# Where SBUF buffers begin: all activation and weight buffers of a one-core decoder block at 32 mod 64 bytes

## The chip, the cores and the metric

The program runs on 1 core of one Trainium2 chip. The metric is device time in microseconds (us) for one execution of the whole block, lower is better. Engines are named as in the profile: PE (matrix multiply), PEld (its weight load), DVE (vector), ACT (scalar), POOL (GpSimd), SP (the queue that issues the DMAs).

## The reference

One decoder block in float32, on 512 tokens of width 1024:

```python
mod = silu(c) @ w_ada + b_ada                 # six vectors of 1024: shift, scale, gate, twice
h = rmsnorm(x, norm_mix_w) * (1 + scale_m) + shift_m
z, xbc, dt, u_pool, gates = split(h @ w_in)   # 2048, 3072, 32, 1024, 2048 columns
y_ssd = rmsnorm_by_group(ssd_scan(silu(conv(xbc)), dt) * silu(z)) @ w_branch_ssd
y_pool = causal_multiscale_pool(u_pool) @ w_branch_pool
x = x + gate_m * ((sigmoid(g1) * y_ssd + sigmoid(g2) * y_pool) @ w_out)
h2 = rmsnorm(x, norm_mlp_w) * (1 + scale_f) + shift_f
x = x + gate_f * (square(relu(h2 @ w_up)) @ w_down)   # hidden width 4096
return rmsnorm(x, norm_final_w)
```

## The kernel before, in words

Activations stand channels on partitions, tokens along the row: a tile is 128 partitions by 512 float32, 2,048 bytes in each partition. Every product of float32 operands is made of three products in float32r: each operand is split in a high and a low part (`split`, L107, for activations; `load_unit`, L120, for weights), and `mm3` (L138) adds `whi·xhi`, `whi·xlo` and `wlo·xhi` (L140, L141, L142) into one PSUM bank. A **unit** (L144) is one column block of 128 of a weight with eight chunks of rows: 24 such matmuls, each with 128x128 weights and 512 columns of a moving tile. The moving tile is always an activation part; the weights are always a slice of an `hl` buffer, except in three blocks of the output projection (L689), whose parts stand in `s` buffers.

The stages follow one another: first norm and first units (L198 to L295), the scan in four groups with other units between its steps (L399 to L600), the gates (L606), the last group's branch projection and pooling mix (L618), the pooling branch's projection (L623), the second gates (L630), the output projection (L681 by whole rows of 512 tokens, L691 by halves of 256), and the MLP (L734 on; the last three blocks by halves, L747).

Buffers come from rings (`Slots`, L40): `s0` to `s49` of 2,048 bytes, `raw0` to `raw3` and `hl0` to `hl7` of 4,096, `xs0`, `xs1`, `sz0`, `sz1` of 8,192, `mt0` to `mt2` of 4,096, and `sm0` to `sm3` of 16 bytes. A ring hands its buffers out in the order in which they came back, so which buffer a tile gets is fixed when the program is built. SBUF addresses are given in the order in which the buffers are first made, each rounded up to 32 bytes. The fixed tiles of L85 to L103 come first; the rings follow when each buffer is first asked for. In the program before, `sm0` (16 bytes, rounded up to 32) is first asked for in the first norm, when `s0` to `s15` have an address and `s16` to `s49` have none. So two families stand in the program:

| buffers | address mod 64 bytes, before | after |
|---|---|---|
| `xs`, `sz`, `raw0`, `s0` to `s15` | 0 | 32 |
| `raw1` to `raw3`, all `hl`, `s16` to `s49`, `mt` | 32 | 32 |
| `cbc`, `ident`, `ones` | 0 | 32 |
| `mod`, `tri` | 32 | 0 |
| `ea`, `dtk`, `ncs`, `cd`, `dec` | 0 | 32 |
| `par_t` | 0 | 0 |

The second row's buffers begin at 288 mod 512 before and at 416 mod 512 after: all of them move by the same 128 bytes. The first row's move by 160 bytes. `s0` to `s15` are called the low buffers below. Of the 24 moving tiles of a unit, the low ones number:

| stage | time in the profile before, us | matmuls of 512 columns | low moving tiles in a unit of 24 |
|---|---|---|---|
| three groups' branch projection, in the scan | 164 to 377 | 24 blocks of 12 | 3 in a block of 12 |
| last group's branch projection | 461 to 479 | 8 blocks of 12 | 6 in a block of 12 |
| pooling branch projection | 505 to 550 | 8 units | 9 |
| second gates | 550 to 593 | 8 units | 0 |
| output projection, first five blocks | 593 to 621 | 5 units | 8 |
| MLP, whole rows | 658 to 979 | 58 units | 7, 9 or 11 |

All other units have none: their moving tiles are `h`, in `s17` to `s39`.

Of the kernel before, what the change touches and what calls it, by code (L numbers as in the profile page):

```python
# [7 lines left out]
F32 = mybir.dt.float32  # L8
# [4 lines left out]
P = 128  # L13
# [7 lines left out]
EPS = 1e-5  # L21
WINS = (2, 4, 8, 16)

# Columns of the packed per-channel parameters.
COLS = {}
_n = 0
for _name, _w in (
# [5 lines left out]
NPAR = _n  # L33
# [4 lines left out]


class Slots:  # L40
    """Buffers of one size, handed out in the order in which they were given back."""

    def __init__(self, make, n):
        self.make = make
# [14 lines left out]
def block_kernel(tc, xT, crow, arow, par, adaT, wstart, wz, wx, wpool_in, wgate, wpw, wbs, wbp, wout, wup, wdn, out):  # L59
# [3 lines left out]
    with (  # L63
# [15 lines left out]
        RAW = slots("raw", NRAW, (P, 1024))  # L79
        HL = slots("hl", NHL, (P, 1024))  # L80
        SM = slots("sm", 4, (P, NC))
        PU, PS = slots("ps", 8, (P, T), psp), slots("ps", 8, (P, T), psp)
        PU.free, PS.free = PU.free[:NPU], PS.free[NPU:]

        par_t = sb.tile([P, NPAR], F32, name="par_t")  # L85

        def col(name, j=0, n=1, rows=P):
            a = COLS[name] + j
# [16 lines left out]
        ecs_d = dr.tile([NH, T], F32, name="ecs_d")  # L105

        def split(src):  # L107
            """A tile of float32 in two parts that float32r holds exactly."""
            hi, lo = S.get(F32R), S.get(F32R)
            act.copy(hi, src)  # L110
            dve.tensor_tensor(lo, src, hi.bitcast(F32), ALU.subtract)  # L111
            return hi, lo
# [5 lines left out]
        urgent = [False]  # L118

        def load_unit(src, n=1024, low=None, at=None, cols=1024):  # L120
            """Blocks of 128 columns of a weight, each in two parts; the buffers are free after their next use."""
            at = at or HL
            with tc.high_priority() if urgent[0] else nullcontext():
                r = RAW.get()
                sp.dma_start(r[:, :n], src)
                blocks, kept = [], []
                for a in range(0, n, cols):
                    w = min(cols, n - a)
                    hi, lo = at.get(F32R), at.get(F32R)
                    act.copy(hi[:, :w], r[:, a:a + w])  # L130
                    (low or dve).tensor_tensor(lo[:, :w], r[:, a:a + w], hi[:, :w].bitcast(F32), ALU.subtract)  # L131
                    blocks += [(hi[:, o:o + P], lo[:, o:o + P]) for o in range(0, w, P)]
                    kept += [hi, lo]
            RAW.put(r)
            at.put(*kept)
            return blocks
# [5 lines left out]
            pe.matmul(ps, wlo, xhi[:, t0:t1], start=False, stop=stop)  # L142

        def unit(src, xs):  # L144
            """One column block of 128 with eight chunks of rows; its bank is the caller's to free."""
            w = load_unit(src)
            ps = PU.get()
            for k in range(8):
                mm3(ps, w[k], xs[k], k == 0, k == 7)
            return ps  # L150

        def ada(j, at=RAW):
            """Modulation of 128 channels: silu(c) . w_ada + b_ada."""
            r = at.get()
            sp.dma_start(r, adaT[j])
            dve.tensor_tensor_reduce(r, r, cbc, 1.0, col("b_ada", j), ALU.mult, ALU.add, mod[:, j:j + 1])  # L156
            at.put(r)

        def column_sums(ps, sqs, c0, c1, opened=False):
            """Sums over the partitions of the tiles' chunks of tokens, tokens on partitions."""  # L160
            if len(sqs) == 1 and not opened:
                for c in range(c0, c1):
                    pe.matmul(ps[:, c:c + 1], sqs[0][:, c * P:(c + 1) * P], ones[:, :1], start=True, stop=True)
                return
            if not opened:
                pe.matmul(ps[:, c0:c1], ones, zeros[:, c0:c1], start=True, stop=False)
            for i, sq in enumerate(sqs):
                for c in range(c0, c1):
                    pe.matmul(ps[:, c:c + 1], sq[:, c * P:(c + 1) * P], ones[:, :1], start=False,
                              stop=i == len(sqs) - 1 and c == c1 - 1)  # L170

        def rstd(sums, n, c0, c1, at):
            """1/sqrt(mean + eps) of those sums, on every partition; the bank is the caller's to free."""
            r, d = SM.get(), at.get()
            act.activation(r[:, c0:c1], sums[:, c0:c1], AF.Sqrt, bias=eps_t, scale=1.0 / n)
            dve.reciprocal(r[:, c0:c1], r[:, c0:c1])
            for c in range(c0, c1):
                dc, rc = d[:, c * P:(c + 1) * P], r[:, c:c + 1]
                if c % 2:
                    act.activation(dc, ident, AF.Copy, scale=rc)  # L180
                else:
                    dve.tensor_scalar(dc, ident, rc, None, ALU.mult)
            bc = PU.get()
            pe.matmul(bc[:, c0 * P:c1 * P], ones, d[:, c0 * P:c1 * P], start=True, stop=True)
            SM.put(r)
            at.put(d)
            return bc

        def modulate(x, R, scale, shift, hi, lo, t0=0, t1=T):
            """x * R * scale + shift, in two parts."""  # L190
            t = S.get()
            dve.scalar_tensor_tensor(t[:, t0:t1], x[:, t0:t1], scale, R[:, t0:t1], ALU.mult, ALU.mult)
            act.activation(hi[:, t0:t1], t[:, t0:t1], AF.Identity, bias=shift)
            dve.scalar_tensor_tensor(
                lo[:, t0:t1], t[:, t0:t1], shift, hi[:, t0:t1].bitcast(F32), ALU.add, ALU.subtract)
            S.put(t)

# [1 line left out]
        dve.memset(ones, 1.0)  # L199
        dve.memset(zeros, 0.0)  # L200
        dve.memset(eps_t, EPS)
# [2 lines left out]
            tri, ones, pattern=[[1, P]], compare_op=ALU.is_ge, fill=0.0, base=0, channel_multiplier=-1)  # L204

        def warm(n):
            """Products of no use that keep the array's clock up."""
            ps = PU.get()
            for _ in range(n):
                pe.matmul(ps[:, :P], ones, ones, start=True, stop=True)  # L210
            PU.put(ps)
# [3 lines left out]
        with tc.manual_schedule():  # L215
# [3 lines left out]
            xs0 = [S.get() for _ in range(8)]  # L219
            for k in range(8):  # L220
                sp.dma_start(xs0[k], xT[k])
            sp.dma_start(par_t, par)
            warm(6)
            act.activation(crow_t, crow_t, AF.Silu)
            cps = [PU.get(), PU.get()]
# [27 lines left out]
            R = rstd(ps, DM, 0, NC, S)  # L253
# [40 lines left out]
        PU.put(*first[8 - NPU:])  # L294
        PS.put(*first[1:8 - NPU])  # L295

# [1 line left out]
        r_ = slice(0, NH)  # L298
        w_ = NC * NH
        v, cs_t, ecs_t = S.get(), S.get(), S.get()  # L300
# [35 lines left out]
        PU.put(tk)  # L336
        S.put(v, cs_t, ecs_t, *tmp)

# [1 line left out]
        def conv(ps, j, o=None):  # L340
            t = S.get()
            w = lambda k: col("conv_w", 4 * j + k)
# [38 lines left out]
        acc = [None] * 8  # L381

        def bs(g, jp):
            """Two column blocks of the SSD branch's projection, the rows of one group."""
            def f():
                w = load_unit(wbs[4 * g + jp])
                for jj in range(2):
                    j = 2 * jp + jj
                    ps = PU.get()
                    for k in range(4):  # L390
                        mm3(ps, w[4 * jj + k], G[g]["y"][k], k == 0, k == 3)
                    if g == 0:
                        acc[j] = S.get()
                        act.copy(acc[j], ps)
                    else:
                        dve.tensor_tensor(acc[j], acc[j], ps, ALU.add)
                    PU.put(ps)
                if jp == 3:
                    free(G[g]["y"])  # L399
            return f  # L400
# [113 lines left out]
            SZ.put(sz)  # L514
            S.put(rg)

# [1 line left out]
        pout = []  # L518
        held = {}

# [50 lines left out]
            u_z(0, i)()  # L571

        def run(g, fillers):
            """One group's scan with other units between its steps."""
            steps = ssd_group(g)
            n = 10
            done = 0
            for k in range(n + 1):
                if k == 9 and g == 3:
                    break  # L580
                alive = next(steps, "end")
                upto = len(fillers) * (k + 1) // (n + 1)
                for f in fillers[done:upto]:
                    f()
                done = upto
                if alive == "end":
                    break
            for f in fillers[done:]:
                f()
            return steps  # L590
# [10 lines left out]
        later = [p_.get() for p_ in (XS, SZ, XS)]  # L601
        F = Slots(lambda i, dt: later[i // 4][:, i % 4, :], 12)

# [1 line left out]
        merged = []  # L605
        for j in range(8):  # L606
            gp = F.get()
# [39 lines left out]
        later = [SZ.get(), SZ.get()]  # L647
        F = Slots(lambda i, dt: later[i // 4][:, i % 4, :], 8)

# [1 line left out]
        x1 = []  # L651
        for j in range(8):
            x = xbig[j // 4][:, j % 4, :]
# [3 lines left out]
        HALVES = ((0, H), (H, T))  # L657

        def residual(ps, j, gate, t0=0, t1=T, sums=True, apart=None):
            """Adds a gated product to x and its squares to the sums."""  # L660
            x = x1[j][:, t0:t1]
            dve.scalar_tensor_tensor(x, ps[:, t0:t1], mod[:, gate + j:gate + j + 1], x, ALU.mult, ALU.add)  # L662
            if not sums:
# [39 lines left out]
        for j in range(45, 48):  # L703
            ada(j)

# [1 line left out]
        def squared(u):  # L707
            dve.tensor_tensor(u, u, u, ALU.mult)  # L708
            p = split(u)
# [8 lines left out]
            return squared(u)  # L718

        def up_first():  # L720
            """The first three units, by halves of the tokens and with the rows' chunks outermost."""
            w = [load_unit(wup[i]) for i in range(3)]
            u = [F.get() for _ in range(3)]
            for t0, t1 in HALVES:
# [107 lines left out]
```

## Time and profile before

| | us |
|---|---|
| median of 3 runs | 1006.45 |
| the runs | 1007.35, 1005.21, 1006.45 |
| span of the profiled execution | 1007.3 |
| the run nearest to that span, taken as the profiled execution's own time | 1007.35 |
| PE busy in the span | 985.8 (98%) |
| DVE busy | 623.2 (62%) |
| ACT busy | 482.6 (48%) |

A busy PE means only that some matmul is in flight: a matmul of 512 columns is shown with some 390 ns, while the next one starts some 230 ns after it. The pace is therefore read from start to start, or from the time that a known number of matmuls takes. In the timeline the first column is the start of an instruction; in a table of stretches the count behind an engine's busy time takes in the one or two instructions that hang over the edges.

### The profile page before, as it was taken

Reading aid. Unit: us, or ns where it says so; the run is one execution under the profiler, and the core shown is the slowest. Engines: PE = TensorE matmul, PEld = TensorE weight load, DVE = VectorE, ACT = ScalarE, POOL = GpSimd, SP = SyncE. Lnnn points to the kernel's source line nnn. Section 1 sums busy time; section 2 is a strip of 40 time slices with the busy share of each in tenths; the row PEclk is TensorE's granted clock in tenths of the full one; section 3 lists DMA queues with packets and bytes.
Section 4 is the critical chain, followed back from the end, with each engine's and each line's share of the span. In section 5 each row is a group of like instructions: output and inputs, shape, how many; then the busy total and the mean of one; then the engine's idle time right before and its main releaser. Section 6 shows DMA issues by size and latency. Waiting matters only on the chain.

```text
span 1007.3 us, 12196 instructions
## 1 busy us (share of the span) xinstructions
PE 985.8 (98%) x4732; PEld 804.1 (80%) x4732; DVE 623.2 (62%) x887; ACT 482.6 (48%) x718; POOL 85.7 (9%) x79
## 2 busy tenths in 40 slices
PE   9799999999999999999999999999999999999997
PEld 7577777878778878788888888988888888888886
DVE  5978777586777776978765655654344334434444
ACT  5277899579648933453422433442133123213342
POOL 3510310211012012210000000000000000000000
PEclk9999999999999999999999999999999999999998
DMA  9725542452344232437886444032323222232302
GB/s 357 273 89 169 145 126 91 123 130 91 94 129 123 89 111 94 133 102 230 266 266 196 154 161 144 2 126 83 105 86 103 97 92 94 94 105 84 105 1 84
DMA packets 58620, 129.55 MB, mean 129 GB/s; under 512 B 4609, under 2 KB 29313, under 8 KB 58562
## 3 DMA queue, kind: packets, MB, share of 16 engines
q1 hardware_dynamic: 58562, 128.77, 40.0%
q8 instruction: 37, 0.61, 0.2%
q14 instruction: 21, 0.17, 0.1%
HBM read 126.53 MB, written 2.23 MB: 128 GB/s over the span
## 4 chain that ended last, share of the span: by engine, by line
PE 76%; ACT 8%; DVE 7%; DMA 4%; issue 2%; POOL 1%; SPq 1%; DVEq 0%; POOLq 0%; ACTq 0%
PE ps L140 24%; PE ps L141 24%; PE ps L142 24%; DMA mt<-cs_d 3%; ACT hl L130 2%; DVE sz L156 1%; DVE xs L156 1%; ACT L432 1%; PE ps L469 1%; ACT L349 1%; PE ps L453 1%; PE ps L280 1%; DVE hl L131 1%; ACT mt L432 1%; PE ps L446 1%
## 5 line engine op out<-in xcount | busy, mean ns | idle before, releaser
L140 PE MATMUL ps<-s,hl 128*128 128x512 f32 (+1 forms) x1272 | 493.4, 388 | 1.3 <-ACT pad L528 1.2
L141 PE MATMUL ps<-s,hl 128*128 128x512 f32 (+1 forms) x1272 | 488.4, 384 | 0.0
L142 PE MATMUL ps<-s,hl 128*128 128x512 f32 (+1 forms) x1272 | 488.2, 384 | 0.0
L130 ACT CAST hl<-raw 128x1024 fp32r<-128x1024 f32 (+1 forms) x161 | 167.2, 1041 | 285.3 <-PE ps L141 282.6
L140 PEld LDWEIGHTS ps<-s,hl 128*128 128x128 f32 x1272 | 238.9, 188 | 53.3 <-issue 3.5
L142 PEld LDWEIGHTS ps<-s,hl 128*128 128x128 f32 x1272 | 239.0, 188 | 50.2 <-issue 1.0
L141 PEld LDWEIGHTS ps<-s,hl 128*128 128x128 f32 x1272 | 239.1, 188 | 49.4 <-issue 1.4
L131 DVE TENSOR_TENSOR hl<-raw,hl 128x1024 fp32r<-128x1024 f32 x153 | 189.1, 1238 | 130.3 <-ACT hl L130 126.0
L662 DVE SCALAR_TENSOR_TENSOR xs<-ps,mod,xs 128x512 f32<-128x512 f32 (+1 forms) x46 | 31.3, 681 | 110.6 <-PE ps L142 110.5
L110 ACT CAST s<-sz 128x512 fp32r<-128x512 f32 x52 | 31.5, 620 | 52.8 <-DVE sz L708 42.1
L156 DVE CUSTOM_DVE_ANT_0 raw<-raw,cbc,par_t 128x1024 f32<-128x1024 f32 x32 | 40.9, 1279 | 21.2 <-DMA raw<-adaT 21.2
L111 DVE TENSOR_TENSOR s<-sz,s 128x512 fp32r<-128x512 f32 x52 | 35.0, 690 | 22.9 <-ACT s L110 22.9
L432 ACT ACTIVATE mt<-mt,ncs 128x128 f32<-128x128 f32 x128 | 41.7, 392 | 13.6 <-POOL mt L428 13.3
L345 DVE SCALAR_TENSOR_TENSOR s<-ps,par_t,s 128x511 f32<-128x511 f32 (+2 forms) x54 | 40.2, 745 | 7.4 <-ACT s L343 6.8
L280 PE MATMUL ps<-s,hl 128*128 128x512 f32 x144 | 35.1, 397 | 6.4 <-ACT s L265 6.4
L428 POOL TENSOR_SCALAR_AFFINE_SELECT mt<-mt 128x1024 f32<-128x1024 f32 x16 | 19.8, 1244 | 218.0 <-ACT cd L425 117.3
L280 PEld LDWEIGHTS ps<-s,hl 128*128 128x128 f32 x144 | 26.2, 188 | 14.7 <-ACT s L265 9.0
L349 ACT ACT_TABLE_LOAD x19 | 24.4, 1283 | 7.4 <-DVE s L345 7.1
L432 ACT ACT_TABLE_LOAD x20 | 25.7, 1283 | 0.3
L492 POOL TENSOR_TENSOR s<-s 128x256 f32<-128x256 f32 x16 | 17.3, 1082 | 67.9 <-ACT s L491 67.9
L491 ACT ACTIVATE s<-sz 128x512 f32<-128x512 f32 x16 | 10.1, 630 | 26.2 <-DVE sz L490 26.2
L110 ACT CAST s<-s 128x512 fp32r<-128x512 f32 x16 | 9.9, 622 | 25.6 <-DVE s L541 25.3
(164 smaller groups left out, 797.7 us busy)
## 6 DMA issues: line engine op xcount, KB each, us to landing
raw<-adaT SPq DMA_DIRECT2D x32, 512.0 KB, 4.3
raw<-wup SPq DMA_DIRECT2D x32, 512.0 KB, 3.3
raw<-wdn SPq DMA_DIRECT2D x32, 512.0 KB, 3.3
raw<-wx SPq DMA_DIRECT2D x18, 512.0 KB, 3.4
raw<-wz SPq DMA_DIRECT2D x16, 512.0 KB, 4.2
mt<-cs_d SPq DMA_DIRECT2D x16, 512.0 KB, 6.2
raw<-wbs SPq DMA_DIRECT2D x16, 512.0 KB, 3.4
raw<-wgate SPq DMA_DIRECT2D x16, 512.0 KB, 4.0
```

Source lines behind the costliest of these rows:

```text
L110: act.copy(hi, src)
L111: dve.tensor_tensor(lo, src, hi.bitcast(F32), ALU.subtract)
L130: act.copy(hi[:, :w], r[:, a:a + w])
L131: (low or dve).tensor_tensor(lo[:, :w], r[:, a:a + w], hi[:, :w].bitcast(F32), ALU.subtract)
L140: pe.matmul(ps, whi, xhi[:, t0:t1], start=start, stop=False)
L141: pe.matmul(ps, whi, xlo[:, t0:t1], start=False, stop=False)
L142: pe.matmul(ps, wlo, xhi[:, t0:t1], start=False, stop=stop)
L156: dve.tensor_tensor_reduce(r, r, cbc, 1.0, col("b_ada", j), ALU.mult, ALU.add, mod[:, j:j + 1])
L280: pe.matmul(first[u], w[u][i // 2], h[k][i % 2], start=k == 0 and i == 0, stop=k == 7 and i == 2)
L345: dve.scalar_tensor_tensor(t[:, sh:], ps[:, :T - sh], w(3 - sh), t[:, sh:], ALU.mult, ALU.add)
L349: act.activation(o, t, AF.Silu)
L432: act.activation(m[:, i, :], m[:, i, :], AF.Exp, bias=ncs[:, c, g * HG + i:g * HG + i + 1])
```

## The change

No instruction is added, removed or moved. On every engine the same instructions stand in the same order with the same waits and the same buffer numbers; only the addresses differ, and the line numbers behind L82 are one higher. The 16-byte tiles get their addresses first, and the tile of the parameters is 8 columns (32 bytes) wider, of which the DMA fills the first 298 as before.

```diff
         SM = slots("sm", 4, (P, NC))
+        SM.put(*[SM.get() for _ in range(4)])
         PU, PS = slots("ps", 8, (P, T), psp), slots("ps", 8, (P, T), psp)
         PU.free, PS.free = PU.free[:NPU], PS.free[NPU:]
 
-        par_t = sb.tile([P, NPAR], F32, name="par_t")
+        par_t = sb.tile([P, NPAR + 8], F32, name="par_t")
...
-            sp.dma_start(par_t, par)
+            sp.dma_start(par_t[:, :NPAR], par)
```

The rest of the diff takes out comments and docstrings.

On PE, at the start of the first unit of the pooling branch's projection (L623), the program before has these rows. The first name behind the arrow is the moving tile, the second the weights; the first number in a name is the buffer, the others count uses.

```order
L140 MATMUL ps0_726_4123<-s45_596_3477,hl0_724_4119 128x512
L141 MATMUL ps0_726_4123<-s10_597_3478,hl0_724_4119 128x512
L142 MATMUL ps0_726_4123<-s45_596_3477,hl1_725_4120 128x512
L140 MATMUL ps0_726_4123<-s31_600_3490,hl0_724_4119 128x512
L141 MATMUL ps0_726_4123<-s49_601_3491,hl0_724_4119 128x512
L142 MATMUL ps0_726_4123<-s31_600_3490,hl1_725_4120 128x512
```

In the changed program the same place reads so.

```order
L141 MATMUL ps0_730_4127<-s45_600_3481,hl0_728_4123 128x512
L142 MATMUL ps0_730_4127<-s10_601_3482,hl0_728_4123 128x512
L143 MATMUL ps0_730_4127<-s45_600_3481,hl1_729_4124 128x512
L141 MATMUL ps0_730_4127<-s31_604_3494,hl0_728_4123 128x512
L142 MATMUL ps0_730_4127<-s49_605_3495,hl0_728_4123 128x512
L143 MATMUL ps0_730_4127<-s31_604_3494,hl1_729_4124 128x512
```

Buffers and order are the same; `s10` begins at 0 mod 64 bytes in the one and at 32 in the other, and all the other tiles of the rows at 32 in both.

## Rows read from the trace of the kernel before

**Rows 1.** The page: span, busy times, granted clock, shares of the chain of waits.

```profile
span 1007.3 us, 12196 instructions
PE 985.8 (98%) x4732; PEld 804.1 (80%) x4732; DVE 623.2 (62%) x887; ACT 482.6 (48%) x718; POOL 85.7 (9%) x79
PEclk9999999999999999999999999999999999999998
PE 76%; ACT 8%; DVE 7%; DMA 4%; issue 2%; POOL 1%; SPq 1%; DVEq 0%; POOLq 0%; ACTq 0%
```

**Rows 2.** Groups of PE's matmuls by line and shape: count, busy us, mean ns.

```profile
L140 PE MATMUL ps<-s,hl 128*128 128x512 f32 x1176 | 466.3, 397 | 1.3 <-ACT pad L528 1.2
L142 PE MATMUL ps<-s,hl 128*128 128x512 f32 x1176 | 461.3, 392 | 0.0
L141 PE MATMUL ps<-s,hl 128*128 128x512 f32 x1176 | 461.1, 392 | 0.0
L280 PE MATMUL ps<-s,hl 128*128 128x512 f32 x144 | 35.1, 397 | 6.4 <-ACT s L265 6.4
...
L141 PE MATMUL ps<-s,hl 128*128 128x256 f32 x96 | 27.2, 284 | 0.0
...
L282 PE MATMUL ps<-s,hl 128*128 128x512 f32 x16 | 4.9, 389 | 0.0
```

**Rows 3.** Stretches: length, busy us (count) by engine, granted clock, DMA share, GB/s.

```profile
core 0: us, PE busy (x) PEld busy (x) DVE busy (x) ACT busy (x) POOL busy (x), PEclk, DMA share, GB/s
...
174.34:177.09 2.75, 2.75 (x13) 2.21 (x12) 0.89 (x1) 2.59 (x9) 0.00 (x0) 1.00 0.73 209
...
461.18:483.21 22.03, 22.03 (x97) 17.85 (x96) 18.93 (x27) 8.00 (x10) 0.00 (x0) 1.00 0.78 251
505.00:549.69 44.69, 44.69 (x194) 36.06 (x193) 28.64 (x43) 10.00 (x11) 0.00 (x0) 1.00 0.75 241
549.69:593.21 43.52, 43.52 (x193) 36.03 (x192) 26.34 (x34) 16.25 (x23) 0.00 (x0) 1.00 0.51 170
593.21:621.10 27.89, 27.89 (x121) 22.45 (x120) 16.44 (x21) 10.60 (x15) 0.00 (x0) 1.00 0.50 150
621.10:629.59 8.49, 8.49 (x73) 8.48 (x72) 4.40 (x7) 2.43 (x4) 0.00 (x0) 1.00 0.18 65
657.66:978.94 321.28, 321.28 (x1395) 261.37 (x1394) 137.27 (x155) 102.33 (x132) 0.00 (x0) 1.00 0.28 92
```

**Rows 4.** Timeline of PE inside one MLP unit: start us, duration us.

```profile
906.98 0.40 PE L140 MATMUL ps<-s,hl 128*128 128x512 f32 x1
...
909.31 0.39 PE L141 MATMUL ps<-s,hl 128*128 128x512 f32 x1
...
911.80 0.39 PE L140 MATMUL ps<-s,hl 128*128 128x512 f32 x1
```

**Rows 5.** Timeline of ACT, four weight casts in a row, in brackets the idle time before.

```profile
701.94 1.05 ACT L130 CAST hl<-raw 128x1024 fp32r<-128x1024 f32 x1 [4.51 <-PE ps L141]
707.51 1.05 ACT L130 CAST hl<-raw 128x1024 fp32r<-128x1024 f32 x1 [4.51 <-PE ps L141]
713.03 1.05 ACT L130 CAST hl<-raw 128x1024 fp32r<-128x1024 f32 x1 [4.47 <-PE ps L141]
718.60 1.05 ACT L130 CAST hl<-raw 128x1024 fp32r<-128x1024 f32 x1 [4.51 <-PE ps L141]
```

**Rows 6.** Timeline of DVE over the same units: the low parts of the weights.

```profile
703.02 1.23 DVE L131 TENSOR_TENSOR hl<-raw,hl 128x1024 fp32r<-128x1024 f32 x1
...
719.68 1.23 DVE L131 TENSOR_TENSOR hl<-raw,hl 128x1024 fp32r<-128x1024 f32 x1
```

**Rows 7.** DMA issues of the page: count, size, median us from issue to landing.

```profile
raw<-wup SPq DMA_DIRECT2D x32, 512.0 KB, 3.3
raw<-wdn SPq DMA_DIRECT2D x32, 512.0 KB, 3.3
```

## The prediction

> **What bounds the kernel now.** I read the page first: the reader is to see that PE is busy for 985.8 of 1007.3 us, at the full granted clock in all slices but the last, and that it holds 76% of the chain of waits [rows 1]. A busy PE is not yet a PE at its peak, so the next view is the pace. The groups by line and shape give the number of matmuls that matter: 3 x 1,176 + 144 + 16 = 3,688 in float32r with 512 columns [rows 2]. Their mean of some 390 ns says nothing of the pace, since they overlap; stretches of known content do.
>
> Two stages that follow each other are the natural experiment. From 549.69 to 593.21 us stand the eight units of the second gates, 192 matmuls whose moving tiles are `h`, all at 32 mod 64 bytes: 43.52 us, or 226.7 ns a matmul and 5.440 us a unit. From 505.00 to 549.69 us stand eight units of the pooling branch's projection, 192 matmuls again, same shapes, the same weight buffers, with 9 of 24 moving tiles in low buffers at 0 mod 64: 44.69 us, 232.8 ns and 5.586 us [rows 3]. In both PE has no gap, the granted clock is 1.00, and DVE and ACT have work for at most 28.64 of 44.69 us. So the difference, 1.17 us, is not a wait for another engine. DMA is busier in the slower one (0.75 against 0.51), which leaves a second reading; the third view removes it. Inside one unit of the MLP the moving tiles come in the order `s11`, `s7`, `s11`, `s15`, `s13`, `s15`, `s25`, `s12`, `s25`, seven of nine low, and then `s17`, `s18`, `s17` and so on to `s30`, none low. The ten matmuls from 906.98 to 909.31 us go at 2.33 / 10 = 233 ns, the eleven that follow, to 911.80 us, at 2.49 / 11 = 226 ns [rows 4]. It is the same unit with the same two weight buffers. The bound of the late stages is PE's own pace, and the pace goes with where the moving tile begins.
>
> **The change, part by part.** It moves addresses alone: the instructions, their order, their waits and their buffers stay. So the cost is that of matmuls whose moving tile goes from 0 to 32 mod 64, plus whatever other operands do at their new places.
>
> The sum takes each stage at the pace of the clean one, 226.67 ns (43.52 / 192), which I take as the pace after since there every moving tile and every weight slice was at 32 mod 64 already [rows 3]:
> - MLP, whole rows: 58 units, 1,392 matmuls. 58 x 5.440 = 315.52 us against 321.28 us now: 5.76 us.
> - Pooling branch's projection: 44.69 - 43.52 = 1.17 us.
> - Output projection, five units: 27.89 - 27.20 = 0.69 us.
> - Last group's branch projection and pooling mix: from 461.18 to 483.21 us start 95 matmuls (97 counted, two of them over the edges), 22.03 us against 95 x 0.22667 = 21.53: 0.50 us.
> - The scan's 24 blocks of 12 with three low tiles: one of them takes 2.75 us against 12 x 0.22667 = 2.72, so 0.03 each and 0.7 us in all. In the scan PE also waits for others, so I count half: 0.35 us.
>
> Together 5.76 + 1.17 + 0.69 + 0.50 + 0.35 = 8.47 us, all on PE's row where it has no gap, so nothing hides it. What could eat it is the supply of weights. A unit's cast takes 1.05 us on ACT after 4.5 us of idle [rows 5], its low part 1.23 us on DVE [rows 6], its load 3.3 us [rows 7]; a unit of 5.44 us still covers each, and the gates ran at 5.44 with this supply and DMA at 0.51 to 0.75. So a unit shorter by 0.07 to 0.15 us makes nothing else late.
>
> The other edits cost nothing. ACT and DVE don't see the shift: four weight casts in a row, which go through `raw0` to `raw3` in turn and so through one source at 0 and three at 32, all take 1.05 us [rows 5], and the matching DVE rows 1.23 us at both ends of the same four units [rows 6]. The three extra handings-out of 16-byte tiles issue nothing, and the parameters' DMA fills the same 298 columns.
>
> One piece the trace does not show: the 432 matmuls of 256 columns (three lines, 96 + 48 of each; the row of one line and form stands for three) [rows 2]. 72 of them take 8.49 us, 117.9 ns each [rows 3], with low tiles on both operands throughout, and no stretch is free of them. Half of 226.67, 113.3 ns, is the best I can price them at, 4.6 ns x 432 = 2.0 us of gain; I let the loss be as large. PEld is busy there for 8.48 of 8.49 us, so the weight load sets that pace rather than the moving tile, and I take 0.
>
> [...]
>
> **The rivals.**
> - *No change.* The slow pace may belong not to the address but to what the low buffers are: they lie at the bottom of the rings, and the tiles in them are fresh results, while `h` is old. Shifting them by 160 bytes then does nothing, 1006.4. For it: every low buffer is both low and at 0 mod 64, so the trace can't part the two. Against it: units of 9 mix high and low buffers filled by the same lines (L110, L111), and in [rows 4] the pace changes inside a unit where only the buffer changes. [...] Chance 0.08.
> - *Part of it.* The slow rhythm may outlast the tile that starts it for some other reason (a change between stages, a new weight), so that units fall only halfway: 8.47 / 2 = 4.2 us, 1002.2. For it: within units of 9 low tiles the others don't reach 226.7 ns either, as 15 x 226.7 + 9 x 234 would be 5.51 us and not 5.586 [rows 3]. Against it: [rows 4], where the pace comes back at once. Chance 0.06.
> - *Slower.* The rule may run over more than 64 bytes. The fast buffers began at 288 mod 512, the new place is 416 mod 512, which no moving tile of the trace has had. If that place is slow, it is slow for everything: the matmuls outside the late stages, 3,688 - 1,392 - 192 - 120 - 95 = 1,889, mostly at 226.7 ns now, go to about 233 [rows 4], 1,889 x 6.3 = 11.9 us; the late units go from 321.28 / 58 = 5.54 [rows 3] to 24 x 0.233 = 5.59, 3 us more. That is 1021. It decides from the point where a place costs more than 2.3 ns a matmul over all 3,688 (8.47 us). Against it: the fast buffers, moving and weights, all move by one and the same 128 bytes, so their places relative to each other stay, and any rule of 128 bytes or less gives the same place. Chance 0.06.
>
> **How the numbers follow.** The forecast, chance 0.80, is the sum. From the profiled execution's own time, 1007.35, it gives 998.9; that execution is 0.9 us above the median of the runs, 1006.45, from which it gives 998.0, and that is my number. Its own range is 995.5 (the 256-column matmuls gain 2.0 and the scan's blocks their other half, 998.0 - 2.35) to 1000.0 (they lose as much); the three runs of before lie 2.1 us apart. For 8 in 10 it needs little more: 995.5 to 1002.5 takes in the partial case. Some 0.2%, 2 us, is what a measurement of this kernel can tell from no change. Faster: 0.80 + 0.06, the forecast and the half. Same: 0.08, the first rival. Slower: 0.06, the third.
>
> **What would show it right or wrong.** Right: the 58 MLP units take 315.5 us from first to last start, the pooling projection's eight 43.5, and the gates' eight still 43.5; casts stay at 1.05 us; the last stage's 256-column matmuls stay near 118 ns. If the gates' units rise above 5.44, the new place is itself slow and the rival of a longer rule holds. If the MLP stays at 321 us with the gates at 43.5, the address never mattered. If PE shows gaps before units in the MLP, the supply of weights has become the bound.

## The result, and the profile after

The changed kernel takes 999.29 us (median of 9 runs, 998.14 to 1001.59) against 1006.54 us (9 runs). The ratio is 0.9925, 95% interval 0.9912 to 0.9938: faster, clear of noise. The forecast was 998.0 with a range of 995.5 to 1002.5.

The profiled spans are 1007.3 us before [rows 1] and 998.8 after, 8.5 us apart, where the sum of the prediction was 8.47. The page of the changed kernel, its span and busy times:

```profile
span 998.8 us, 12196 instructions
PE 977.2 (98%) x4732; PEld 805.1 (81%) x4732; DVE 623.8 (62%) x887; ACT 482.5 (48%) x718; POOL 84.8 (8%) x79
PEclk9999999999999999999999999999999999999998
PE 77%; ACT 8%; DVE 7%; DMA 4%; issue 2%; POOL 1%; SPq 0%; DVEq 0%; POOLq 0%; ACTq 0%
```

PE's busy time falls by 8.6 us; the others move by 1.0 us at most (PEld, 804.1 to 805.1). The stages of [rows 3], in the changed kernel; the columns are length, PE's busy time with its count, granted clock, DMA share, GB/s:

```profile
core 0: us, PE busy (x), PEclk, DMA share, GB/s
460.15:481.70 21.55, 21.55 (x96) 1.00 0.76 253
503.46:546.98 43.52, 43.52 (x193) 1.00 0.77 242
546.98:590.50 43.52, 43.52 (x193) 1.00 0.51 170
590.50:617.95 27.45, 27.45 (x122) 1.00 0.46 153
617.95:626.58 8.63, 8.63 (x74) 1.00 0.20 64
654.82:970.37 315.55, 315.55 (x1394) 1.00 0.28 94
```

From the top, against the kernel before: the last group's branch projection and pooling mix 22.03 to 21.55 us, the pooling branch's projection 44.69 to 43.52, the gates unchanged at 43.52, the output projection 27.89 to 27.45, 72 matmuls of 256 columns 8.49 to 8.63, the 58 MLP units 321.28 to 315.55. The pooling projection still runs with DMA at 0.77, so the traffic was no part of its slow pace. ACT's weight cast stays at 1.05 us (compare [rows 5]):

```profile
698.39 1.05 ACT L131 CAST hl<-raw 128x1024 fp32r<-128x1024 f32 x1 [4.39 <-PE ps L142]
```

### The profile page after: what moved, and what is told of

Read it like the earlier page. It is cut to its first block, busy times and chain, and to the rows that moved or that the text cites. A ratio compares the mean times of both kernels' runs of the same rounds, so it can differ in the third digit from the quotient of the medians.

```text
span 998.8 us, 12196 instructions
## 1 busy us (share of the span) xinstructions
PE 977.2 (98%) x4732; PEld 805.1 (81%) x4732; DVE 623.8 (62%) x887; ACT 482.5 (48%) x718; POOL 84.8 (8%) x79
## 4 chain that ended last, share of the span: by engine, by line
PE 77%; ACT 8%; DVE 7%; DMA 4%; issue 2%; POOL 1%; SPq 0%; DVEq 0%; POOLq 0%; ACTq 0%
PE ps L141 24%; PE ps L142 23%; PE ps L143 23%; DMA mt<-cs_d 4%; ACT hl L131 2%; DVE sz L157 1%; DVE xs L157 1%; ACT L433 1%; PE ps L470 1%; PE ps L454 1%; PE ps L211 1%; ACT L350 1%; PE ps L281 1%; PE ps L447 1%; DVE hl L132 1%
```

## The experiments

All kernels compute the whole block with the same instructions in the same order; only addresses differ. "In step" below means that the weights and the moving tile of a matmul begin at the same place, counted first mod 64 bytes; mod what it has to be counted is a question of the later runs. The granted clock is 1.00 in every stretch shown; for a unit of 24 matmuls of 512 columns, 5.44 us means 226.7 ns each, and 5.60 us means 233.3 ns.

**Whose place counts: four runs on one chip.** The prediction spoke of where the moving tile begins. But in the kernel before, all weights begin at 32 mod 64, so "at 32" and "in step with the weights" could not be told apart.

```diff
 e1_all0: the 16-byte tiles first, parameters' tile as before
+        SM.put(*[SM.get() for _ in range(4)])
```

> Half of the change alone: the 16-byte tiles first, the parameters' tile as before, so that every activation and weight buffer begins at 0 mod 64. Theory A (absolute: a 512-column float32r matmul whose moving tile begins at 0 mod 64 takes 232 to 234 ns whatever else stands where): all 3,688 of them go slow, a unit of 24 takes 5.58 to 5.62 us in every stage, the gates' eight units 44.7 to 44.9 instead of 43.5, the span rises from the 998.8 us of the changed kernel by some 3,688 x 6.3 ns = 23 to about 1022. Theory B (relative: slow where moving tile and weights differ mod 64) and theory C (mixture: slow where moving tiles of both places alternate in one stream) both say that it is as fast as the changed kernel: units of 5.440, span about 999.

```diff
 e2_mirror: the parameters' tile wider, 16-byte tiles as before
-        par_t = sb.tile([P, NPAR], F32, name="par_t")
+        par_t = sb.tile([P, NPAR + 8], F32, name="par_t")
```

> The other half alone: the parameters' tile wider, the 16-byte tiles where they were, so that the families swap: s0 to s15 begin at 32 mod 64, s16 to s49 and all weights at 0. Theory A (absolute): the gates' units, whose moving tiles now all begin at 0, go from 5.44 to about 5.6 us; the MLP's, with 13 to 17 of 24 at 0, to some 5.6; span about 1020. Theory B (relative): as the kernel before, since every pair of moving tile and weights differs or agrees as it did: gates 5.44, MLP 5.51 to 5.58, span 1007. Theory C (mixture): the same as B.

```diff
 e3_m32w0: the changed kernel, and behind the fixed tiles
+        S.put(*[S.get() for _ in range(NSLOT)])
+        sb.tile([P, NC], F32, name="shift_t")
```

> All s buffers (every moving tile) at 32 mod 64, all hl, raw, xs, sz, mt at 0. Theory A (absolute, moving tile): as the changed kernel, units of 5.440 and span about 999. Theory B (relative): all units with hl weights slow, about 5.6 us each, span about 1020. Theory C (mixture of moving tiles): fast, about 999. The last stage's 256-column matmuls, 117.6 ns in the kernel before and 120.0 in the changed one, go back to about 117.6 here if it is the agreement of weights and moving tile that costs there.

```diff
 e4_m0w32: e1_all0, and behind the fixed tiles
+        S.put(*[S.get() for _ in range(NSLOT)])
+        sb.tile([P, NC], F32, name="shift_t")
```

> All s buffers (every moving tile) at 0 mod 64, all hl, raw, xs, sz, mt at 32. Theory A (absolute): every unit about 5.6 us, span about 1020. Theory B (relative): the same, about 1020, since weights and moving tiles differ everywhere. Theory C (mixture of moving tiles): fast, units of 5.440, about 999.

The medians are of 4 runs, of e2_mirror of 10.

| kernel | moving tiles, weights (mod 64) | median us | ratio to before (95%) |
|---|---|---|---|
| e1_all0 | 0, 0 | 999.46 | 0.9909 (0.9893 to 0.9926) |
| e2_mirror | 32 or 0 mixed, 0 | 1007.98 | 1.0004 (0.9994 to 1.0014) |
| e3_m32w0 | 32, 0 | 1017.01 | 1.0087 (1.0072 to 1.0102) |
| e4_m0w32 | 0, 32 | 1018.16 | 1.0102 (1.0086 to 1.0118) |

Three stretches of each: the gates, the 58 MLP units, and the last stage's first 72 matmuls of 256 columns. The kernel before has 43.52 and 321.28 us in the first two [rows 3]; its third is

```profile
978.94:987.40 8.46, 8.46 (x73) 1.00 0.00 0
```

With everything at 0:

```profile
547.86:591.38 43.52, 43.52 (x193) 1.00 0.52 170
655.68:971.23 315.55, 315.55 (x1394) 1.00 0.29 94
971.23:979.86 8.63, 8.63 (x73) 1.00 0.00 0
```

The mirror image of the kernel before:

```profile
548.39:591.92 43.53, 43.53 (x194) 1.00 0.51 169
656.33:977.60 321.27, 321.27 (x1394) 1.00 0.28 92
977.60:986.07 8.47, 8.47 (x74) 1.00 0.00 0
```

Moving tiles at 32 and weights at 0:

```profile
551.92:596.72 44.80, 44.80 (x193) 1.00 0.51 165
661.41:986.21 324.80, 324.80 (x1395) 1.00 0.28 91
986.21:994.74 8.53, 8.53 (x74) 1.00 0.00 0
```

Moving tiles at 0 and weights at 32:

```profile
555.50:600.30 44.80, 44.80 (x193) 1.00 0.51 165
664.99:989.78 324.79, 324.79 (x1394) 1.00 0.28 91
989.78:998.31 8.53, 8.53 (x73) 1.00 0.00 0
```

Theory A falls at the first block: moving tiles at 0 are as fast as at 32 when the weights are there too, and A's 1022 us is missed by 22. Theory C falls with the last two: uniform moving tiles, out of step, run at 44.80 / 192 = 233.3 ns throughout. Theory B gave all four signs and, for the mirror, the time of the kernel before to 0.01 us in the MLP. Half of the change alone, the tiles of 16 bytes first, does the whole of it; the other half alone does nothing. What the kernel needed was one family of addresses for weights and moving tiles together; 32 mod 64 has no merit of its own.

**Weights or the other engines' buffers, and how far apart: four runs.** In the two slow kernels `raw`, `xs`, `sz` and `mt` had gone along with the weights.

```diff
 e5_hl0: the changed kernel; hl alone goes to 0 mod 64
+        S.put(*[S.get() for _ in range(NSLOT)])
+        sb.tile([P, 8], F32, name="shift_a")
+        HL.put(*[HL.get() for _ in range(NHL)])
+        sb.tile([P, 8], F32, name="shift_b")
 e7_diff64: the changed kernel; all but s goes 64 bytes on
+        S.put(*[S.get() for _ in range(NSLOT)])
+        sb.tile([P, 16], F32, name="shift_a")
 e8_diff16: weights begin 16 bytes into wider buffers (e9_diff48: and these 32 bytes on)
-        HL = slots("hl", NHL, (P, 1024))
+        WIDE = slots("hl", NHL, (P, 1040))
+        HL = Slots(lambda i, dt: WIDE.make(i, dt)[:, 4:1028], NHL)
...
```

> As the changed kernel (all s, raw, xs, sz, mt at 32 mod 64), with the eight hl buffers alone at 0. Theory B (what counts is whether a matmul's weights and its moving tile begin at the same place mod 64): every unit 24 x 233.3 = 5.60 us, span about 1015 to 1018, as when raw, xs, sz and mt went along. Rival B' (what counts is the moving tile against the buffers that ACT and DVE read and write meanwhile, which went along with the weights in the two runs before): units stay at 5.44 us, span about 999.

> All s buffers at 32 mod 128, all hl, raw, xs, sz, mt at 96 mod 128: weights and moving tiles begin at the same place mod 64 and 64 bytes apart mod 128. Theory B with a period of 64: units of 5.440 us, span about 999. Rival with a period of 128: between that and the 32-byte case, units of 5.5 to 5.6, span 1005 to 1018.

> As the changed kernel, with the parts of the weights beginning 16 bytes into wider hl buffers: weights at 48, moving tiles at 32 mod 64. A step at any disagreement: units of 5.60 us, span about 1016. A rule of 32-byte halves: both begin in the same half, 5.44 us, span about 999. In proportion to the distance: 5.52 us, span about 1008.

> Weights at 16, moving tiles at 32 mod 64, 48 bytes apart one way and 16 the other. A step at any disagreement: units of 5.60 us, span about 1016. A rule of 32-byte halves: they begin in different halves, 5.60 us, span about 1016. In proportion to the shorter distance: 5.52 us, about 1008; to the distance one way: 5.68 us or the reverse of the 16-byte case.

Medians and ratios: e5_hl0 1017.78 us, 1.0097 (1.0074 to 1.0119); e7_diff64 1017.71, 1.0095 (1.0068 to 1.0122); e8_diff16 1015.68, 1.0078 (1.0054 to 1.0102); e9_diff48 1011.33, 1.0030 (1.0016 to 1.0045). The gates and the MLP with `hl` at 0 mod 64 and the rest at 32:

```profile
553.51:598.31 44.80, 44.80 (x193) 1.00 0.51 165
663.00:987.80 324.80, 324.80 (x1395) 1.00 0.28 91
```

and with weights 64 bytes from the moving tiles:

```profile
554.87:599.67 44.80, 44.80 (x193) 1.00 0.51 165
664.30:989.09 324.79, 324.79 (x1394) 1.00 0.28 91
```

So I had the period wrong: 64 bytes apart is as slow as 32, and "the same place mod 64" is not the rule. This touches the first question too. In e5_hl0 the two shifts add up, and `raw`, `xs`, `sz` and `mt` stand 64 bytes on as well, so it does not part them from the weights. Two other runs do. In e8_diff16 those four begin where the moving tiles do, at 416 mod 512, and all units are slow (5.57 to 5.59 us in the gates); in e10_diff128s below they begin 128 bytes off, and the units with weights in step are fast (5.46 us). So it is the weights, and the places of the buffers that ACT and DVE touch besides are no part of it. The runs with 16 and 48 bytes were badly built for their question: the wider buffers are 4,160 bytes long, so each stands 64 bytes (mod 512) further than the last, and high and low part of a weight had different distances. Their units take 5.57 to 5.59 and 5.54 to 5.56 us; no step, half or proportion is shown by them, and the 1011 us of the second is a time that none of the expectations gave.

**The period: three kernels**, each with four distances, one by pair of weight buffers.

```diff
 e10_diff128s, e11_below: GAPS sets the distance of each pair of hl
+        S.put(*[S.get() for _ in range(NSLOT)])
+        for i in range(4):
+            if GAPS[i]:
+                sb.tile([P, GAPS[i] // 4], F32, name=f"gap{i}")
+            HL.put(*[HL.get() for _ in range(2)])
...
 e12_odd16: hl one row of 32 bytes longer, weights 16 bytes in, high parts placed first
+        WIDE = slots("hl", NHL, (P, 1032))
+        HL = Slots(lambda i, dt: WIDE.make(i, dt)[:, 4:1028], NHL)
...
```

> Moving tiles at 416 mod 512 as in the changed kernel; the four pairs of weight buffers begin 0, 128, 256 and 384 bytes (mod 512) above them, so every fourth unit shows one distance. Period of 128: all units 5.440 us. Period of 256: the pairs at 0 and 256 give 5.440, those at 128 and 384 about 5.60. Only the same place mod 512 is fast: one unit in four at 5.440, the others 5.60. Span in that order about 999, 1008, 1013.

> Moving tiles at 416 mod 512; the four pairs of weight buffers begin 96, 416, 448 and 480 bytes (mod 512) above them, the last three being 96, 64 and 32 bytes below. In all slow runs so far the weights stood 16 to 64 bytes above. If only equality is fast, all four give units of 5.60 us, span about 1017. If weights below the moving tile are free, three pairs give 5.44 and the one at 96 gives 5.60, span about 1003.

> Moving tiles at 416 mod 512; high and low part of a weight alike begin 16, 48, 80 or 112 bytes above them, by pair. In the two runs with shifts of 16 and 48 bytes the high and the low part stood at different distances, and single matmuls came out between 229 and 234 ns, 1015.7 and 1011.3 us in all. If any inequality costs the same, all four pairs give units of 5.60 us, span about 1017. If those two were faster by a real effect of the 16-byte offset, some pairs lie between 5.44 and 5.60, and the span between 1005 and 1014.

One run each: 1008.42 us beside 1008.83 for the kernel before on the same chip, 1016.12 and 1017.31 beside the same; the reading rests on the units, not on these single times. The second expectation says that the weights stood 16 to 64 bytes above in all slow runs so far, and that is wrong: in e8_diff16 and e9_diff48, whose buffers stand 64 bytes further each, the weights stood up to 464 and 496 bytes above the moving tiles. Four units of the gates in a row, at distances 128, 256, 384 and 0 bytes:

```profile
554.81:560.40 5.59, 5.59 (x25) 1.00 0.64 204
560.40:565.86 5.46, 5.46 (x25) 1.00 0.32 98
565.86:571.45 5.59, 5.59 (x25) 1.00 0.27 95
571.45:576.91 5.46, 5.46 (x26) 1.00 0.33 104
```

at 416, 448, 480 and 96 bytes (the first three are 96, 64 and 32 below):

```profile
558.68:564.29 5.61, 5.61 (x25) 1.00 0.61 193
564.29:569.80 5.51, 5.51 (x26) 1.00 0.30 97
569.80:575.39 5.59, 5.59 (x25) 1.00 0.28 95
575.39:581.01 5.62, 5.62 (x25) 1.00 0.36 100
```

and at 48, 80, 112 and 16 bytes:

```profile
559.24:564.84 5.60, 5.60 (x25) 1.00 0.61 198
564.84:570.40 5.56, 5.56 (x25) 1.00 0.32 96
570.40:576.00 5.60, 5.60 (x25) 1.00 0.29 95
576.00:581.60 5.60, 5.60 (x25) 1.00 0.37 109
```

The fast distances are 0 and 256. The 0.02 us that these units lie above 5.44 stand at their ends, beside units out of step: in the last one the first three steps take 229, 232 and 231 ns and the last one 233. There is no free side below. All other distances lie between 5.51 and 5.62; two of them (64 below with 5.51, 80 above with 5.56) are cheaper than the rest, which take 5.59 to 5.62, and why is open.

So the rule repeats at 256 bytes among the distances tried. The two badly built runs bear this out. In them `hl0` and `hl1` stand 256 bytes from `hl4` and `hl5`, and `hl2` and `hl3` from `hl6` and `hl7`. A unit with `hl0` takes 5.60 us on the mean in e8_diff16 and one with `hl4` the same, one with `hl2` 5.58 and one with `hl6` the same; in e9_diff48 these are 5.56 and 5.54 (24 to 26 units of each, those under 5.8 us).

**Which of the matmuls is slowed: one run.**

```diff
 e13_lo128: the changed kernel; low parts of the weights 128 bytes on
+        S.put(*[S.get() for _ in range(NSLOT)])
+        HL.free = [0, 2, 4, 6, 1, 3, 5, 7]
+        HL.put(*[HL.get() for _ in range(4)])
+        sb.tile([P, 32], F32, name="gap")
+        HL.put(*[HL.get() for _ in range(4)])
+        HL.free = list(range(NHL))
```

> Moving tiles and the high parts of the weights at 416 mod 512 as in the changed kernel, the low parts 128 bytes above, so that of each three matmuls the first two (L140, L141) have weights in step with the moving tile and the third (L142) has not. If what collides is the reading of the next weights with the moving tile now streaming, the time from L141 to L142 is long (233 ns) and the two others 227. If it is a matmul's own weights, the time from L142 to the next L140 is long. Both give units of 8 x (2 x 226.7 + 233.3) = 5.49 us and a span of about 1004. If one pair out of step slows its neighbours as well, units of 5.55 to 5.60, span 1010 to 1016.

1009.97 us, beside 1007.73 for the kernel before. The timeline of PE in an MLP unit; L147 and L148 are the two products with the high part, L149 the one with the low part:

```profile
702.62 0.39 PE L147 MATMUL ps<-s,hl 128*128 128x512 f32 x1
702.85 0.40 PE L148 MATMUL ps<-s,hl 128*128 128x512 f32 x1
703.08 0.40 PE L149 MATMUL ps<-s,hl 128*128 128x512 f32 x1
703.32 0.39 PE L147 MATMUL ps<-s,hl 128*128 128x512 f32 x1
703.54 0.40 PE L148 MATMUL ps<-s,hl 128*128 128x512 f32 x1
703.78 0.40 PE L149 MATMUL ps<-s,hl 128*128 128x512 f32 x1
704.01 0.39 PE L147 MATMUL ps<-s,hl 128*128 128x512 f32 x1
```

From each start to the next, over all 512-column units of this run, a step takes 227.2 ns at L147, 232.5 at L148 and 233.8 at L149 (means of 1,133, 1,167 and 1,130 steps, those under 0.3 us). So one matmul with weights out of step costs about 13 ns (5.8 and 7.1 over 226.7), in its own step and the one before it. Neither of the two simple versions expected that. The third, that a neighbour suffers, names it, and the unit of 8 x (227.2 + 232.5 + 233.8) = 5.55 us is at the lower end of what it expected. The weight loads of the same stretch:

```profile
702.85 0.19 PEld L149 LDWEIGHTS ps<-s,hl 128*128 128x128 f32 x1
703.09 0.19 PEld L147 LDWEIGHTS ps<-s,hl 128*128 128x128 f32 x1
```

The weights out of step are loaded while L148 runs, so their reading could be what slows that step. While L149 runs, weights in step are loaded, and it is slow all the same. The reading of the next weights is thus not the whole of it; what slows a step is open.

## Why the prediction was right, and where it was not

- *The bound, and the pace as the place to look*: right. The two stages read as a natural experiment, 226.7 against 232.8 ns, became equal at 43.52 us.
- *The sum*: right in all, partly because its errors cancel. It is 8.47 us against 8.5 in the profiled spans; the medians differ by 7.25, and the interval of the ratio, 6.2 to 8.9 us, holds both. On the chip of the first four experiments, e1_all0 with the same paces is 8.4 below the kernel before (999.46 and 1007.89). By terms: MLP 5.76 against 321.28 - 315.55 = 5.73; pooling projection 1.17 against 1.17; last group 0.50 against 0.48; output projection 0.69 against 0.44, since its first unit waits and keeps its 5.66 us, so a wait stood in a term that I had priced as pace; the scan 0.35 against 1.0, since the last group's projection begins at 454.24 instead of 455.28 us; the 256-column matmuls 0 against a loss of 0.4. In the scan the blocks gained most of what I had halved, and one wait came out shorter by 0.5, PE's idle time before the product of L453 in one block (1.05 to 0.58 us), which another execution need not repeat: that part is luck.
- *The profiled execution's own time*: misread. In every later run a time is 1.7 us above the span of its profile (1000.5 and 998.8 for the changed kernel). A span of 1007.3 thus belongs to some 1009.0 us, which none of the three runs has. The forecast went from the median, so its number does not hang on this.
- *The 256-column matmuls at nothing*: wrong, a loss within its bounds. The first 72 went from 117.9 to 119.9 ns (8.49 to 8.63 us), and the two stretches that hold all 432 grew by 0.31 and 0.07 us (36.56 to 36.87 and 28.36 to 28.43): 248 of the 432 stood in step before already. The step that failed is "no stretch is free of them". From 653.34 to 657.66 us the kernel before has 36 of these matmuls with moving tiles `s20` to `s30` and weights all at 32 mod 64, at 4.32 / 36 = 120.0 ns, which prices the loss:

```profile
653.34:657.66 4.32, 4.32 (x38) 1.00 0.01 4
```

  The reason given, that the weight load sets that pace rather than the moving tile, does not hold as it stands: the pace moved where only places did. With `hl` out of step with the moving tiles they go at 118.5 ns (8.53 us for 72, in e3_m32w0). So the two widths want opposite things, and the mixed layout of before had helped there.
- *"The pace goes with where the moving tile begins"*: wrong as a cause. It held for this change only because all weights stood at 32 already. The sum was safe because it used a stage in which both stood alike and the change makes every stage so. The sentence that the fast buffers, weights and moving tiles, all move by the same 128 bytes was the one that carried it.
- *The rivals.* "No change", that low buffers are slow for what they hold, is out: in the changed kernel the same tiles in the same low buffers go at full pace, and in e3_m32w0 and e4_m0w32 the gates, whose moving tiles are `h` in the other buffers, take 44.80 us instead of 43.52. "Slower", a rule longer than 64 bytes, was closer to the truth than its chance: the rule repeats at 256 bytes, but it is relative, and the common shift kept it. "Part of it" had its premise right: the slow pace outlasts the tile that starts it. Two slowed steps a low tile are not enough for a unit of 9 (9 x 13 ns = 0.12 us against 5.586 - 5.440 = 0.146). In the pooling unit at 505.00 us, after `s45`, `s10`, `s45`, six steps with the moving tiles `s31`, `s49`, `s31`, `s44`, `s41`, `s44`, all in step, take 1.39 us or 232 ns each, though only the last of them stands before a low tile; in [rows 4] the pace is back after two more steps. What decides how long it lasts is open. The change leaves no tile to start it, so nothing fell only halfway. The six steps lie between these two rows of the kernel before:

```profile
505.69 0.39 PE L140 MATMUL ps<-s,hl 128*128 128x512 f32 x1
...
507.08 0.40 PE L140 MATMUL ps<-s,hl 128*128 128x512 f32 x1
```

One version could still beat the changed kernel. Everything in step is the best place found for 3,688 of the 4,120 float32r matmuls; to put the 432 narrow ones out of step needs weight buffers of their own, for an estimated 1 us at most (432 x 2.4 ns, from 8.46 against 8.63 us for 72 of them). It was not tried.

## What to carry to other kernels

When one kind of matmul shows two paces in one trace, sort its instructions by buffer and look at addresses: a tile of 16 bytes made in the middle of the buffers had put 16 of the activation buffers 32 bytes out of step with the weights and cost 0.75%. For float32r matmuls of 512 columns put weights and moving tiles at the same place mod 256 bytes (here 5.44 to 5.46 us a unit, against 5.51 to 5.62 at the other distances tried), make small tiles first, and compare stages of equal shape before calling a busy engine fully used. And vary the partner operand before naming the one that changed: the right number here came with the wrong cause.

## What the runs showed of the hardware

- A float32r matmul of 128x128 weights and 512 columns takes 226.7 ns when weights and moving tile begin at the same place mod 256 bytes (units of 5.44 us in the changed kernel, where all are in step; 5.46 at distances of 0 and 256 bytes in e10_diff128s, between units out of step), and 229.6 to 234.2 at the other distances tried (units of 5.51 to 5.62 us). 32 bytes apart it is 233.3 ns (44.80 us for 192 in e3_m32w0). The slow pace can outlast the matmul out of step by several steps (six of 232 ns in the pooling unit).
- With 256 columns it is 119.9 ns in step (8.63 us for 72) and 117.5 to 118.5 in the mixed and the 32-byte layouts (8.46 to 8.53): the opposite sign. In step, two matmuls of 256 columns take 13 ns more than one of 512 (2 x 119.9 - 226.7).
- ACT's weight cast takes 1.05 us on the mean whether `hl` begins in step with `raw` (the changed kernel) or 32 bytes from it (e5_hl0); DVE's subtraction for the low part takes 1.24 and 1.25.
